# Second copies of keys and values for the other 64 partitions: loaded again, or copied by GpSimd

## The chip, the core and the metric

The kernel runs on one core of a Trainium2 chip. The metric is the device time of one execution in microseconds. A core has five engines, each with its own queue that it works off in order: TensorE (PE; its weight loads are shown as PEld), VectorE (DVE), ScalarE (ACT), GpSimd (POOL) and SyncE (SP). SP does nothing but issue transfers; GpSimd both computes and issues transfers, and both take their place in the same queue.

## What is computed

One layer of a decoder on 1024 tokens of 1024 channels. A combined input projection feeds a sliding-window attention with sinks, a gated linear recurrence and several gates; both branches are projected, merged, projected again and added to the input. The part that the change touches is the attention, 16 heads of 64 channels in 4 groups (one key and value head each), with a window of 128 tokens:

```python
s = jnp.einsum('bnqkgd,bnskd->bnkgqs', qb, kb) * (1.0 / math.sqrt(hd))
band = (diff >= 0) & (diff < WINDOW)
s = jnp.where(mask[None, :, None, None], s, -1e30)
m = jnp.maximum(jnp.max(s, axis=-1, keepdims=True), sink)
p = jnp.exp(s - m)
denom = jnp.sum(p, axis=-1, keepdims=True) + jnp.exp(sink - m)
o = jnp.einsum('bnkgqs,bnskd->bnqkgd', p / denom, vb)
```

All matmul operands are split into a high and a low part in fp32r, so that a product is made of three matmuls.

## The kernel before

The input projection runs in pieces of 12 matmuls (`piece()`, into banks `bk` of PSUM, later the recurrence's projection into `rp`). Into its last part the attention is woven: a loop over 35 *turns* u, of which turn u begins the block u (128 tokens of a group of four heads) and carries the two blocks before it further. TensorE's order in a turn is fixed by the order in which the code is written: `scores(u)` (tile `s_ps`, 8 matmuls of q against keys `ks`), the pieces, `values(u - 3)` (tile `pv`: weights `phc` and `plc` against `vb`, and `cm` against `vd`), `transposed(u - 2)` (tile `pt`), and then `scores(u + 1)`. `s_ps`, `pt` and `pv` have one buffer each.

Behind a transposition come, each on its own engine and in this order: ScalarE's cast `phc` (`split_a`), VectorE's difference `plc` (`split_d`), and two selects of GpSimd (`masks`), which write the halves of `cm` from `phc` and `plc`: partitions 64 to 127 of `cm` come from partitions 0 to 63 of `plc`. GpSimd's other work in a turn is `sink(u + 1)`, a small copy into the tile `p`, which waits for the transposition that frees the buffer.

A *pair* m is the two turns 2m and 2m+1, which share their keys, queries and values:

- `load_k(m)` writes `ks`, 64 channels in partitions 0 to 63 and the same again in 64 to 127 (the queries hold high parts in the one half and low parts in the other), in two transfers on SP's queue. It is called at the end of `scores(2m - 3)`.
- `load_v(m)` writes `vb` and `vd` in four transfers of 64 partitions on GpSimd's queue. In `vb` the upper half is the lower one shifted by one block of 64 tokens; in `vd` both halves are the same. It is called in `values(2m - 4)`, that is in turn 2m - 1, behind the masks of turn 2m - 2.

Stores of earlier results, such as `smr_d`, are on GpSimd's queue as well, where the pieces issue them: each waits for the ScalarE operation (`c`, L810) that makes its data.

Of the kernel before, what the change touches and what calls it, by code (L numbers as in the profile page):

```python
# [52 lines left out]
def tile_hybrid_block(ctx, tc, x, x_t, pk, rows, posr, posi, c_row, w_ss, w_gate, w_main, w_v,  # L53
                      w_g, w_ap, w_rp, w_out, out):
    nc = tc.nc
    V, A, G, T = nc.vector, nc.scalar, nc.gpsimd, nc.tensor

    def dma(dst, src, eng=nc.sync):
        dst, src = (a.bitcast(F32) if a.dtype == F32R else a for a in (dst, src))
        return eng.dma_start(dst, src)  # L60

    def f32(ap):
        return ap.bitcast(F32)
# [65 lines left out]
    vs_d = [tc.dram_tile([64, 18, P], F32, name=f"vs_d{g}") for g in range(NG)]  # L129
    dv_d = [tc.dram_tile([64, 18, P], F32, name=f"dv_d{g}") for g in range(NG)]  # L130
# [19 lines left out]
    for kc in range(KC):  # L150
        for lst, nm in ((hh, "hh"), (hl, "hl")):
            if kc < 4:
                a = hba.tile([P, HALF], F32R, name=f"{nm}a{kc}")
                b = b12.tile([P, HALF], F32R, name=f"{nm}b{kc}")
                lst.append([a[:], b[:]])
            else:
                a = hb.tile([P, S], F32R, name=f"{nm}{kc}")
# [641 lines left out]
    def flush():  # L799
        while behind:  # L800
            behind.pop(0)()
# [438 lines left out]

    at_ctx, psx_ctx = ExitStack(), ExitStack()
    at = psx = None
    U = {}

    def open_attn():
        nonlocal at, psx
# [14 lines left out]
    def load_k(m):  # L1261
        g, t0 = m // 4, (m % 4) * 256
        ks = at.tile([P, 2, 384], F32R, tag="ks", name="ks", bufs=2)
        kv = k_d.rearrange("(b a r j) t -> j (a r) b t", b=2, a=2, r=32, j=4)[g]
        lo = P if t0 == 0 else 0
        for rep in range(2):
            dma(ks[rep * 64:(rep + 1) * 64, :, lo:], kv[:, :, t0 - P + lo:t0 + 256])
        U["k", m] = ks

    def load_q(m):  # L1270
        g, t0 = m // 4, (m % 4) * 256
        qs = at.tile([P, 4, 256], F32R, tag="qs", name="qs", bufs=2)
        if g < 2:
            dma(qs[:], q_d[g][t0 // 64:t0 // 64 + 4].rearrange("x (a j) q -> a x (j q)", j=4))
        else:
            src = q_d[g].rearrange("(a j) t -> a j t", j=4)
            for i in range(4):
                dma(qs[:, i, :].rearrange("a (j q) -> a j q", j=4),
                    src[:, :, t0 + 64 * i:t0 + 64 * i + 64])
        U["q", m] = qs  # L1280

    def load_v(m):
        g, i0 = m // 4, m % 4 * 4
        vb = at.tile([P, 4, P], F32R, tag="vb", name="vb", bufs=3)
        vd = at.tile([P, 4, P], F32R, tag="vd", name="vd", bufs=3)
        for e in range(2):
            half = slice(64 * e, 64 * e + 64)
            dma(vb[half], vs_d[g][:, i0 + e:i0 + e + 4, :], G)
            dma(vd[half], dv_d[g][:, i0 + 2:i0 + 6, :], G)
        U["v", m] = vb, vd  # L1290

    def sink(u):
        px = at.tile([P, 4, P + 1], F32, tag="p", name="p", bufs=3)
        U["p", u] = px, at.tile([P, 2, 4], F32, tag="small", name="small", bufs=4)
        gs = W["sink"][:, u // 8 * 2:u // 8 * 2 + 2]
# [10 lines left out]
    def scores(u):  # L1306
        g, n = u // 8, u % 8
        ks, qs = U["k", u // 2], U["q", u // 2]
        s_full = psx.tile([P, 1024], F32, tag="s", name="s_ps")
        s_ps = s_full[:].rearrange("p (j k) -> p j k", j=4)  # L1310
        for j in range(4):
            h = j // 2
            t0 = (n % 2) * P + 64 * h
            first = 0 if n else P - 64 * h
            w = qs[:, n % 2 * 2 + h, j % 2 * P:j % 2 * P + P]
            for b in range(2):
                W["pe"] = T.matmul(s_ps[:, j, first:192], w, ks[:, b, t0 + first:t0 + 192],  # L1317
                                   start=(b == 0), stop=(b == 1))
        U["s", u] = s_ps, *U.pop(("p", u))
        if n % 2 and u // 2 + 2 < 16:  # L1320
            load_k(u // 2 + 2)
            load_q(u // 2 + 2)

    def maxima_a(u):
        s_ps, px, sm = U["s", u]
        if u % 8:
            A.copy(px[:, :, 0:P], s_ps[:, :, 0:P])
        else:
            A.copy(px[:, 2:4, 64:P], s_ps[:, 2:4, 64:P])

    def maxima_d(u):
        s_ps, px, sm = U["s", u]
        V.copy_predicated(px[:, :, 0:64], W["mle"][:].unsqueeze(1).to_broadcast([P, 4, 64]),
                          s_ps[:, :, P:192])
        V.tensor_reduce(out=sm[:, 0, :], in_=px[:], axis=AX.X, op=ALU.max, negate=True)

    def weights_a(u):
        s_ps, px, sm = U["s", u]
        for j in range(4):
            A.activation(px[:, j, :], px[:, j, :], AF.Exp, bias=sm[:, 0, j:j + 1],  # L1340
                         accum_out=sm[:, 1, j:j + 1])

    def weights_d(u):
        s_ps, px, sm = U["s", u]
        p, den = px[:, :, 0:P], sm[:, 1, :]
        V.reciprocal(den, den)
        V.tensor_tensor(out=p, in0=p, in1=den.unsqueeze(2).to_broadcast([P, 4, P]),
                        op=ALU.mult)

    def transposed(u):  # L1350
        px = U.pop(("s", u))[1]
        pt = psx.tile([P, 4, P], F32, tag="t", name="pt")
        for j in range(4):
            W["pe"] = T.transpose(pt[:, j, :], px[:, j, 0:P], ident[:])  # L1354
        U["t", u] = [pt]
# [6 lines left out]
    def split_d(u):  # L1362
        pt, phc = U.pop(("t", u))
        plc = at.tile([P, 4, P], F32R, tag="plc", name="plc")
        V.tensor_tensor(out=plc[:], in0=pt[:], in1=f32(phc[:]), op=ALU.subtract)
        U["m", u] = phc, plc
# [11 lines left out]
    def values(u):  # L1378
        vb, vd = U["v", u // 2]
        phc, plc, cm = U.pop(("m", u))  # L1380
        pv = psx.tile([P, 4, P], F32, tag="v", name="pv")
        prods = [(vb, m, h) for m in (phc, plc) for h in range(0 if u % 8 else 1, 2)]
        prods += [(vd, cm, h) for h in range(2)]
        for i, (b, m, h) in enumerate(prods):
            js = slice(2 * h, 2 * h + 2)
            W["pe"] = T.matmul(pv[:, js, :], b[:, u % 2 * 2 + h, :], m[:, js, :],  # L1386
                               start=(i == 0), stop=(i >= len(prods) - 2),
                               skip_group_check=True)
        if u % 2 == 0 and u // 2 + 2 < 16:
            load_v(u // 2 + 2)  # L1390
        U["pv", u] = [pv[:].rearrange("p (h a) (e q) -> p a e h q", h=2, e=2)]

    def join_a(u):
        pvv = U["pv", u][0]
        ob = at.tile([P, 2, P], F32, tag="ob", name="ob")
        obv = ob[:].rearrange("p a (h q) -> p a h q", h=2)
        A.copy(obv[0:64], pvv[64:128, :, 0])
        A.copy(obv[64:128], pvv[0:64, :, 1])
        U["pv", u].append(ob)
# [272 lines left out]
    def piece():  # L1672
        nonlocal left
        left -= 1
        next(more)

    late, high, loaded = [], [], {}
    for u in range(32 + 3):
        todo = (left - KEEP + (35 - u) // 2) // (35 - u)
        if u < 32:  # L1680
            scores(u)
            maxima_a(u)
            maxima_d(u)
            if u == 0:
                load_k(1)
                load_q(1)
                load_v(0)
            if u == 1:
                load_v(1)
        if 1 <= u < 33:  # L1690
            weights_a(u - 1)
        low = [steps_[2] for steps_ in high]
        while high:
            high.pop(0)[1]()
        for _ in range(todo):
            piece()
        flush()
        if 1 <= u < 33:
            weights_d(u - 1)
        if u >= 3:  # L1700
            values(u - 3)
            join_a(u - 3)
        if u >= 3:
            join_d(u - 3)
        if 2 <= u < 34:
            transposed(u - 2)
            split_a(u - 2)
            split_d(u - 2)
        if u + 1 < 32:
            sink(u + 1)()  # L1710
        if 2 <= u < 34:
            masks(u - 2)
        if "hpool" in W:
            for f in low:
                f()
            if late and ("gq", late[0]) in U and u >= loaded[late[0]] + 2:
                high.append(a_prep(late.pop(0)))
                high[0][0]()
        do_later()
        if u == 26:  # L1720
            outs(1)
        if u >= 3 and u % 2 == 0:
            late.append((u - 3) // 2)
        if u >= 2 and len(loaded) < 16 and len(loaded) <= (u - 2) // 2 and (
                len(loaded) - (late[0] if late else (u - 2) // 2) < 2):
            m = len(loaded)
            load_gq(m)
            loaded[m] = u
# [314 lines left out]
    for i in range(3):  # L2043
        f = fs[i]
# [8 lines left out]
    f = small()  # L2053
# [92 lines left out]
```

## Time and profile before

| what | value |
|---|---|
| time, median of 3 runs | 910.77 us (909.4 to 911.3) |
| time of the profiled execution | 906.86 us |
| its span | 905.1 us |
| TensorE busy | 882.7 us (98%) |
| VectorE busy | 721.7 us (80%) |
| ScalarE busy | 553.7 us (61%) |
| GpSimd busy | 183.4 us (20%) |
| moved by DMA | 183.12 MB, 202 GB/s over the span |

The attention's turns lie between 558 and 729 us of the span. In a row of the timeline the first number is the start in us, the second the duration in us, then the engine, the line of the kernel, the operation, what it writes and reads, its shape and how many instructions the row merges; a bracket gives the idle time of that engine just before, and what ended it. In a row of a group the bar separates the name and count from the busy time in us, the mean duration in ns, and the idle time before. DMA rows give the size of a transfer and the median time from its issue to its landing in us. Matmuls overlap, so the duration of a single one is longer than its share of the time.

### The profile page before, as it was taken

The page shows a single profiled execution, that of the slowest core. Times are in us where ns is not written, and L with a number is a line of the kernel's source. Part 1 is how long each engine was busy: PE and PEld are TensorE (multiplying, and loading weights), DVE is VectorE, ACT ScalarE, POOL GpSimd, SP SyncE. Part 2 cuts the span into 40 slices and gives each one's busy share as a digit, 9 for nine tenths or more (in the row PEclk, how much of TensorE's full clock was granted, in tenths as well). Part 3 has the DMA queues.
Part 4 walks back from the last instruction along what each step waited for, and adds up shares of the span by engine and source line. Part 5 has one row for each costly group of instructions (what it writes and reads, how often), then busy time and mean ns, then how long its engine had stood idle before and what let it go on. Part 6 is the DMA issues. An engine that isn't in the chain of part 4 may idle for free.

```text
span 905.1 us, 12954 instructions
## 1 busy us (share of the span) xinstructions
PE 882.7 (98%) x4235; PEld 737.6 (81%) x4235; DVE 721.7 (80%) x1166; ACT 553.7 (61%) x1099; POOL 183.4 (20%) x309
## 2 busy tenths in 40 slices
PE   5999999999999999999999999998999999999997
PEld 3879888888888788878887888887888888888886
DVE  7988798888669974986698476898999846779875
ACT  6754675554566746674777685877888631114555
POOL 0130232210110000000100003565665421310002
PEclk9999999999999999999999999999999999999999
DMA  9951885972534451344244246899889369869314
GB/s 350 414 187 63 292 248 194 311 246 93 181 134 139 149 200 34 137 148 170 104 164 169 82 152 208 280 330 296 222 229 259 122 209 328 297 253 325 141 47 185
DMA packets 99445, 183.12 MB, mean 202 GB/s; under 512 B 31329, under 2 KB 44129, under 8 KB 99378
## 3 DMA queue, kind: packets, MB, share of 16 engines
q1 hardware_dynamic: 86912, 144.52, 47.1%
q0 software_dynamic: 12176, 37.47, 12.5%
q8 instruction: 33, 0.54, 0.2%
q10 hardware_dynamic: 290, 0.32, 0.1%
q14 instruction: 34, 0.28, 0.1%
HBM read 127.37 MB, written 55.28 MB: 202 GB/s over the span
## 4 chain that ended last, share of the span: by engine, by line
PE 70%; DMA 11%; issue 8%; DVE 5%; ACT 4%; POOL 2%; SPq 0%; DVEq 0%; POOLq 0%; ACTq 0%
PE bk L707 39%; PE bo L1918 8%; PE rp L175 7%; PE pgate L1003 5%; DMA yl<-yl_d 3%; PE pmain L175 2%; PE s_ps L1317 2%; DMA r<-w_main 2%; PE pv L1386 2%; DMA wq<-w_out 2%; DMA hl<-yl_d 1%; DMA wq_d<-wq 1%; PE pt L1354 1%; PE bk L175 1%; DVE wl L110 1%
## 5 line engine op out<-in xcount | busy, mean ns | idle before, releaser
L707 PE MATMUL bk<-nh,wl 128*128 128x512 f32 x368 | 143.7, 390 | 0.4 <-DVE wl L110 0.4
L707 PE MATMUL bk<-nh,wh 128*128 128x512 f32 x368 | 143.3, 390 | 0.0
L707 PE MATMUL bk<-nl,wh 128*128 128x512 f32 x368 | 143.2, 389 | 0.0
L707 PEld LDWEIGHTS bk<-nh,wl 128*128 128x128 f32 x368 | 69.1, 188 | 16.1 <-DVE wl L110 1.9
L110 DVE TENSOR_TENSOR wl<-r,wh 128x512 fp32r<-128x512 f32 x112 | 81.4, 740 | 0.0
L707 PEld LDWEIGHTS bk<-nh,wh 128*128 128x128 f32 x368 | 69.1, 188 | 14.4
L707 PEld LDWEIGHTS bk<-nl,wh 128*128 128x128 f32 x368 | 69.1, 188 | 14.1
L60 POOL DMA_DIRECT2D wq_d<-wq x32 | 21.9, 684 | 270.4 <-DVE wq L1191 255.4
L104 ACT CAST wh<-r 128x512 fp32r<-128x512 f32 x112 | 68.0, 617 | 9.0 <-DMA r<-w_ap 6.3
L707 PE MATMUL bk<-hh,wl 128*128 128x512 f32 x184 | 71.7, 390 | 0.1
L707 PE MATMUL bk<-hh,wh 128*128 128x512 f32 x184 | 71.6, 389 | 0.0
L707 PE MATMUL bk<-hl,wh 128*128 128x512 f32 x184 | 71.6, 389 | 0.0
L110 DVE TENSOR_TENSOR wl<-ws,wh 128x512 fp32r<-128x512 f32 x80 | 54.5, 684 | 4.2 <-ACT wh L104 4.2
L1340 ACT ACTIVATE p<-p,small 128x129 f32<-128x129 f32 x128 | 50.1, 401 | 0.0
L104 ACT CAST wh<-ws 128x512 fp32r<-128x512 f32 x80 | 48.2, 614 | 2.9 <-PE bk L1570 2.7
L810 ACT ACTIVATE c<-bk 128x512 f32<-128x512 f32 x31 | 18.5, 597 | 44.3 <-PE bk L707 42.3
L707 PEld LDWEIGHTS bk<-hh,wl 128*128 128x128 f32 x184 | 34.5, 188 | 7.7 <-DVE wl L112 0.5
L707 PEld LDWEIGHTS bk<-hh,wh 128*128 128x128 f32 x184 | 34.6, 188 | 7.2
L707 PEld LDWEIGHTS bk<-hl,wh 128*128 128x128 f32 x184 | 34.5, 188 | 7.0
L1918 PE MATMUL bo<-wh,sum 128*128 128x512 f32 x128 | 39.6, 389 | 0.0
L1317 PE MATMUL s_ps<-ks,qs 128*128 128x192 f32 (+2 forms) x256 | 35.5, 281 | 2.1 <-DMA qs<-q_d 1.4
L707 PE MATMUL bk<-hha,wl 128*128 128x512 f32 x92 | 36.0, 392 | 0.6 <-DVE wl L110 0.6
(420 smaller groups left out, 2336.5 us busy)
## 6 DMA issues: line engine op xcount, KB each, us to landing
r<-w_main SPq DMA_DIRECT2D x100, 256.0 KB, 4.2
wada<-w_ss SPq DMA_DIRECT2D x16, 512.5 KB, 9.2
wq_d<-wq POOLq DMA_DIRECT2D x24, 256.0 KB, 3.0
wr<-wq_d SPq DMA_DIRECT2D x24, 256.0 KB, 4.8
ks<-k_d SPq DMA_DIRECT2D x24, 192.0 KB, 3.5
wg<-w_gate SPq DMA_DIRECT2D x8, 512.0 KB, 6.2
sma_d<-c POOLq DMA_DIRECT2D x16, 256.0 KB, 3.9
sgr_d<-c SPq DMA_DIRECT2D x16, 256.0 KB, 2.2
```

The costliest lines, as they stand in the source:

```text
L60: return eng.dma_start(dst, src)
L104: A.copy(dst[0][:], src)
L110: V.tensor_tensor(out=dst[1][:], in0=src, in1=f32(dst[0][:]), op=ALU.subtract)
L175: mm = T.matmul(ps[hf], ww, xx[kc][hf], start=(kc == first and ww is w_h and xx is xh), stop=(kc == last and xx is xl))
L707: W["pe"] = T.matmul(ps, ww[:, c], b[kc][xx_], start=(first and kc == 0 and i == 0), stop=(kc == 3 and i == 2), skip_group_check=not first)
L810: A.activation(t["t"], s(), AF.Tanh, scale=0.5)
L1003: W["pe"] = T.matmul(ps[:, SL[hf]], ww[:, c0:c0 + P], xx_[:, SL[hf]], start=(ic == 0 and i == 0), stop=(ic == 1 and i == 2))
L1317: W["pe"] = T.matmul(s_ps[:, j, first:192], w, ks[:, b, t0 + first:t0 + 192], start=(b == 0), stop=(b == 1))
L1340: A.activation(px[:, j, :], px[:, j, :], AF.Exp, bias=sm[:, 0, j:j + 1], accum_out=sm[:, 1, j:j + 1])
L1354: W["pe"] = T.transpose(pt[:, j, :], px[:, j, 0:P], ident[:])
L1386: W["pe"] = T.matmul(pv[:, js, :], b[:, u % 2 * 2 + h, :], m[:, js, :], start=(i == 0), stop=(i >= len(prods) - 2), skip_group_check=True)
L1918: T.matmul(bank[p][i] if dst is None else dst, a[:, ts_], b[:][:, sl], start=(new and kc == 0 and j == 0), stop=(kc == 3 and j == 2), skip ...
```

## The change

For the pairs from m = 2 on, `load_k` loads only the first 64 partitions, and a GpSimd copy makes the others; `load_v` loads the first half of `vb` and `vd`, and of the second half of `vb` only the last of its four blocks, and two GpSimd copies make the rest. The copies are not issued where the loads are, but kept in a table `twice` by turn: the keys' copy in turn 2m - 1, those of the values in turn 2m + 2, in both cases behind `split_d` and ahead of `sink` and `masks`.

```diff
@@ load_k
-        for rep in range(2):
+        for rep in range(2 if m < 2 else 1):
             dma(ks[rep * 64:(rep + 1) * 64, :, lo:], kv[:, :, t0 - P + lo:t0 + 256])
+        if m > 1:
+            twice.setdefault(2 * m - 1, []).append(
+                lambda: G.tensor_copy(ks[64:128, :, lo:], ks[0:64, :, lo:]))
@@ load_v
-        for e in range(2):
-            half = slice(64 * e, 64 * e + 64)
-            dma(vb[half], vs_d[g][:, i0 + e:i0 + e + 4, :], G)
-            dma(vd[half], dv_d[g][:, i0 + 2:i0 + 6, :], G)
+        a, b = slice(0, 64), slice(64, 128)
+        dma(vb[a], vs_d[g][:, i0:i0 + 4, :], G)
+        dma(vd[a], dv_d[g][:, i0 + 2:i0 + 6, :], G)
+        if m < 2:
+            dma(vb[b], vs_d[g][:, i0 + 1:i0 + 5, :], G)
+            dma(vd[b], dv_d[g][:, i0 + 2:i0 + 6, :], G)
+        else:
+            dma(vb[b, 3, :], vs_d[g][:, i0 + 4, :], G)
+            twice.setdefault(2 * m + 2, []).extend([
+                lambda: G.tensor_copy(vb[b, 0:3, :], vb[a, 1:4, :]),
+                lambda: G.tensor_copy(vd[b], vd[a])])
@@ the loop over turns, between split_d(u - 2) and sink(u + 1)
+        for f in twice.pop(u, ()):
+            f()
```

GpSimd's queue in an odd turn and the even one behind it, for m = 5 (turns 9 and 10; `vb<-vs_d` and `vd<-dv_d` are the transfers of `load_v`). Before:

```order
L60 DMA vb<-vs_d_90 64x512
L60 DMA vd<-dv_d_94 64x512
L60 DMA vb<-vs_d_90 64x512
L60 DMA vd<-dv_d_94 64x512
L1301 COPY p<-sink 128x4
L1372 AFFINE_SELECT cm<-phc 64x512
L1372 AFFINE_SELECT cm<-plc 64x512
L1301 COPY p<-sink 128x4
L1372 AFFINE_SELECT cm<-phc 64x512
L1372 AFFINE_SELECT cm<-plc 64x512
```

And after:

```order
L60 DMA vb<-vs_d_90 64x512
L60 DMA vd<-dv_d_94 64x512
L60 DMA vb<-vs_d_90 64x128
L1270 COPY ks<-ks 64x768
L1311 COPY p<-sink 128x4
L1382 AFFINE_SELECT cm<-phc 64x512
L1382 AFFINE_SELECT cm<-plc 64x512
L1298 COPY vb<-vb 64x384
L1299 COPY vd<-vd 64x512
L1311 COPY p<-sink 128x4
L1382 AFFINE_SELECT cm<-phc 64x512
L1382 AFFINE_SELECT cm<-plc 64x512
```

The keys' copy stands behind three transfers of the values, and the values' copies (those of the pair m = 4) stand ahead of the next sink copy and masks.

TensorE's queue at the end of turn 5 and the start of turn 6, with what its instructions wait for (DMAHW and DMASW are transfers of SP and of GpSimd, Pool is GpSimd). Before:

```order
L1386 MATMUL pv<-cm,vd 128x256 [waits DMASW6_49,DMASW0_49,Pool_49]
L1386 MATMUL pv<-cm,vd 128x256
L1354 MATMUL pt<-ident,p 128x128 [waits PE_49]
L1354 MATMUL pt<-ident,p 128x128 x3
L1317 MATMUL s_ps<-ks,qs 128x192 [waits DMAHW1_49,DMAHW2_49,DMAHW0_49,DVE_49]
```

And after:

```order
L1396 MATMUL pv<-cm,vd 128x256 [waits DMASW6_49,DMASW0_49,Pool_49]
L1396 MATMUL pv<-cm,vd 128x256
L1364 MATMUL pt<-ident,p 128x128 [waits PE_49]
L1364 MATMUL pt<-ident,p 128x128 x3
L1327 MATMUL s_ps<-ks,qs 128x192 [waits DMAHW0_49,DMAHW7_49,DVE_49,Pool_49]
```

The order on TensorE is the same; the scores of an even turn wait for one transfer less, and for GpSimd.

More of the change, by code (lines that the diff above doesn't have):

```diff
@@ L1242, in tile_hybrid_block @@
     at = psx = None
-    U = {}
+    U, twice = {}, {}
     def open_attn():
```

## The prediction

> **What bounds the kernel now.** I read the page's head first, then busy times by stretch, then TensorE's gaps, then one turn row by row.
>
> ```profile
> span 905.1 us, 12954 instructions
> PE 882.7 (98%) x4235; PEld 737.6 (81%) x4235; DVE 721.7 (80%) x1166; ACT 553.7 (61%) x1099; POOL 183.4 (20%) x309
> ```
>
> The whole program is bound by TensorE; GpSimd is busy for a fifth of it. The change touches only the attention stage, so its two halves are what counts (columns: start:end, length, then busy time and count of PE, PEld, DVE, ACT, POOL, granted clock, DMA share, GB/s).
>
> ```profile
> 560.00:640.00 80.00, 75.65 (x454) 65.94 (x453) 68.30 (x129) 64.69 (x207) 43.20 (x79) 1.00 0.93 280
> 640.00:720.00 80.00, 79.64 (x490) 70.73 (x489) 74.07 (x143) 68.12 (x222) 44.47 (x78) 1.00 0.78 220
> ```
>
> In the first half the DMA engines are 93% busy and TensorE loses 4.35 us; in the second it loses 0.36 us, at clock 1.00 in both. VectorE is idle for 11.7 and 5.93 us. These are all of TensorE's gaps there, with what ended each:
>
> ```profile
> 578.97 0.50 PE L1386 MATMUL pv<-cm,vd 128*128 128x256 f32 x2 [0.72 <-POOL cm L1372]
> 594.27 0.51 PE L1386 MATMUL pv<-cm,vd 128*128 128x256 f32 x2 [0.37 <-POOL cm L1372]
> 600.66 1.14 PE L1317 MATMUL s_ps<-ks,qs 128*128 128x192 f32 x8 [0.66 <-DVE p L1333]
> 616.89 1.11 PE L1317 MATMUL s_ps<-ks,qs 128*128 128x192 f32 x8 [1.41 <-DMA qs<-q_d]
> 621.50 0.73 PE L175 MATMUL rp<-yl,wh 128*128 128x512 f32 x2 [1.14 <-DMA yl<-yl_d]
> 718.07 0.50 PE L1386 MATMUL pv<-cm,vd 128*128 128x256 f32 x2 [0.36 <-POOL cm L1372]
> ```
>
> Loads cause 2.55 us of it. That is all that fewer bytes can win here, and the six gaps together, 4.66 us, are the most that any change of this stage's waits can win.
>
> **The change part by part: transfers removed.** For each of the 14 pairs of turns m = 2 to 15 one of the two loads of ks, the second load of vd and three quarters of the second load of vb go.
>
> ```profile
> ks<-k_d SPq DMA_DIRECT2D x24, 192.0 KB, 3.5
> vd<-dv_d POOLq DMA_DIRECT2D x32, 128.0 KB, 4.9
> ```
>
> That is 192 + 128 + 96 = 416 KB for a pair (352 KB for the three pairs with shorter keys), some 5.6 MB in all. Turns 9 and 12 begin with the s_ps at 600.66 and 616.89, so a pair takes 10.8 us there; at the first half's 280 GB/s 0.43 MB are 1.5 us of it, 14%. Some six pairs' loads lie ahead of the two load waits, 8 to 9 us of transfers, so I let both go: -2.55 us. SP issues one ks load less in a pair, which only lets its queue run earlier; GpSimd issues three v loads instead of four.
>
> **The ks copy.** It stands in GpSimd's queue in turn u = 2m-1, behind the masks of turn 2m-2 and behind the three v loads, and s_ps of turn 2m, the next thing that TensorE does after that turn's pv and pt, now waits for it. Turn 19 (m = 10) shows where that is: rows of four engines in order of the path, from the pt of turn 18 to the s_ps of turn 20.
>
> ```profile
> 651.58 0.60 PE L1354 MATMUL pt<-ident,p 128*128 128x128 f32 x4
> 653.50 0.69 DVE L1365 TENSOR_TENSOR plc<-pt,phc 128x512 fp32r<-128x512 f32 x1
> 654.32 0.98 POOL L1372 TENSOR_SCALAR_AFFINE_SELECT cm<-plc 64x512 fp32r<-64x512 f32 x1 [0.41 <-DVE plc L1365]
> 655.26 0.52 POOL L60 DMA_DIRECT2D vb<-vs_d  x1
> 655.77 0.53 POOL L60 DMA_DIRECT2D vd<-dv_d  x1
> 656.30 0.52 POOL L60 DMA_DIRECT2D vb<-vs_d  x1
> 656.82 0.52 POOL L60 DMA_DIRECT2D vd<-dv_d  x1
> 657.38 0.50 POOL L1301 COPY p<-sink 128x4 f32<-128x4 f32 x1
> 656.49 1.12 PE L1317 MATMUL s_ps<-ks,qs 128*128 128x192 f32 x8
> ```
>
> The loads' issues hold GpSimd one after the other: the sink copy starts only when the fourth is out. Three issues end at 655.26 + 1.57 = 656.83, already behind s_ps at 656.49, before the copy has begun. So the copy is not hidden here, whatever it costs.
>
> Its cost is not in the trace. The nearest rows are GpSimd's own:
>
> ```profile
> L1372 POOL TENSOR_SCALAR_AFFINE_SELECT cm<-plc 64x512 fp32r<-64x512 f32 x32 | 30.7, 959 | 16.6 <-DVE plc L1365 16.3
> L1372 POOL TENSOR_SCALAR_AFFINE_SELECT cm<-phc 64x512 fp32r<-64x512 f32 x32 | 21.2, 661 | 23.3 <-ACT phc L1359 23.2
> L1301 POOL COPY p<-sink 128x4 f32<-128x4 f32 x32 | 7.3, 230 | 25.4 <-PE pt L1354 23.0 <-issue 1.8
> L2033 POOL TENSOR_TENSOR xo<-xo,fg_bc 128x512 f32<-128x512 f32 x2 | 2.6, 1301 | 87.0 <-DMA out<-xo 87.0
> ```
>
> A select of 64x512 with one input, which also writes another half of the partitions in the plc form, takes 0.66 us undisturbed; the tiny copy shows some 0.2 us of fixed cost, which leaves 0.86 ns an element. A copy of 768 elements then takes 0.2 + 0.66, about 0.87 us, one of 512 (m = 4, 8, 12) 0.65 us. Bounds: 0.65 us for 768 (the select's whole time, if a copy streams a third faster), and 1.95 us (one and a half times the two-input operation's 1.30). I take 0.87, from the one-input row. The Trainium skill, GPSIMD Engine Reference, section 4.1, says that GpSimd runs one-input work at roughly line rate; as an estimate with the 1.2 GHz clock of its section 1, 768 elements would be 0.64 us, and the sum below some 2.5 us smaller. The select agrees in rate (0.86 ns an element).
>
> The stall of s_ps in a pair is therefore: start of the v loads + 1.57 + 0.87 - start of s_ps. The first three pairs, from the same two engines:
>
> ```profile
> 574.18 0.56 POOL L60 DMA_DIRECT2D smr_d<-c  x1 [1.82 <-ACT c L810]
> 574.74 0.53 POOL L60 DMA_DIRECT2D vb<-vs_d  x1
> 573.90 1.11 PE L1317 MATMUL s_ps<-ks,qs 128*128 128x192 f32 x8
> 584.84 0.53 POOL L60 DMA_DIRECT2D vb<-vs_d  x1
> 584.46 1.11 PE L1317 MATMUL s_ps<-ks,qs 128*128 128x192 f32 x8
> 594.44 0.53 POOL L60 DMA_DIRECT2D vb<-vs_d  x1 [0.22 <-issue]
> 594.97 1.09 PE L1317 MATMUL s_ps<-ks,qs 128*128 128x64 f32 x8
> ```
>
> - m = 2: GpSimd is held by the smr_d store, which waits for a ScalarE result of this very turn, so the v loads start behind s_ps: 574.74 + 2.44 - 573.90 = 3.28 us.
> - m = 3, held in the same way: 584.84 + 2.44 - 584.46 = 2.82 us.
> - m = 4 (512 elements): 594.44 + 2.22 - 594.97 = 1.69 us.
>
> For the other eleven (m = 5 to 15) the distance from the first v load to s_ps lies between these two, the longest (m = 7) and the shortest (m = 15):
>
> ```profile
> 626.47 0.52 POOL L60 DMA_DIRECT2D vb<-vs_d  x1
> 627.94 1.12 PE L1317 MATMUL s_ps<-ks,qs 128*128 128x192 f32 x8
> 703.87 0.53 POOL L60 DMA_DIRECT2D vb<-vs_d  x1
> 704.67 0.56 PE L1317 MATMUL s_ps<-ks,qs 128*128 128x192 f32 x3
> ```
>
> At 1.47 us of distance the stall is 0.97 us (0.75 with 512 elements), at 0.80 it is 1.64 (1.42). Nine long and two short copies give 10.2 us at the one end, 17.6 at the other. The short distances come from plc being late on VectorE, and a TensorE that stops once in a pair lets VectorE catch up; the 3.7 us from pt (651.58) to the mask's end (655.30) in the rows above hold the shortest form of that path, and it stays. I take 11.5 us, near the lower end. The stall recurs in every pair, since the path starts again at a pt that TensorE issues after the last stall.
>
> **The vb and vd copies.** Turn 2m+2 gets two, of 384 and 512 elements: 0.53 + 0.65 = 1.18 us, ahead of sink and masks. Ahead of the sink copy GpSimd mostly waits for pt (23.0 us in its row above), and that covers them: nothing. The exception is turn 6 (m = 2), where two smr_d stores leave no such wait: its masks end some 0.4 us later, and the gap at 594.27 grows and the copy for m = 4 starts later by as much: +0.4 us. Without that cover they would cost up to 1.18 us in each of 14 turns.
>
> **What the stalls take in.** While TensorE waits for a ks copy, what it later waited for gets done. The 0.72 us at 578.97 (masks some 0.3 us later, TensorE 3.3 us later) and the 0.66 us at 600.66 go; with the two loads -3.93 us.
>
> **VectorE and GpSimd together.** One weight preparation of VectorE, alone and beside a GpSimd mask:
>
> ```profile
> 599.56 0.68 DVE L110 TENSOR_TENSOR wl<-r,wh 128x512 fp32r<-128x512 f32 x1
> 654.71 1.14 DVE L110 TENSOR_TENSOR wl<-r,wh 128x512 fp32r<-128x512 f32 x1
> ```
>
> The second runs beside the mask of 654.32: it loses 0.46 us, and that mask takes 0.98 instead of 0.66. The 42 copies will cause more of this. The Trainium skill, SBUF — State Buffer, section "SBUF: two separate sides", says that VectorE work with two SBUF inputs and GpSimd work share a port pair as an exclusive lock, held for a whole instruction. The trace agrees: 1.14 against 0.68 us, and 0.98 against 0.66. By that rule alone the time would be that of the second rival below. In my sum this costs nothing, because each pair grows by more than 1 us and VectorE gets that as slack; as a bound of its own it is a rival.
>
> **Sum.** 3.28 + 2.82 + 1.69 + 0.4 + 11.5 - 3.93 = +15.8 us. The profiled execution took 906.86 us (span 905.1): 922.7. The median of the runs, 910.77, is 3.9 us above that execution, so the median after should be about 926 us.
>
> **Rivals.**
> - *The transfers decide (faster).* If the ks copy got in front of s_ps, the two load waits would go and nothing come back: 910.8 - 2.55 = 908.2; with 0.66 and 0.72 us more, 907. For it: DMA at 93% in the first half. Against: three issues alone end behind s_ps in turn 19. It decides only where masks end some 1 us earlier. 6 in 100.
> - *VectorE becomes the bound instead.* If the queue's stall were small and each copy held VectorE like a mask does, the second half would get 25 copies (turns 20 and 30 begin at 656.49 and 704.67, so 80 us hold 8.3 pairs of three) x 0.46 = 11.5 us against 5.93 us of idle time: +5.6; the first half's 18 copies (8.3 us) fit in its 11.7. With the loads' -2.55: +3 us, about 914. It begins where a copy costs VectorE more than 0.24 us. 7 in 100.
> - *Slow copies.* At 1.95 us instead of 0.87 for 768 elements, and 1.30 instead of 0.65, eleven and three of them add 13.8 us: 940. 8 in 100, as the tail of my own case.
> - *Gains and stalls cancel*: within 0.2%, 3 in 100.
>
> **Numbers.** My case, the queue's stall, has 84 in 100, its slow tail included; its own range is 918 to 940: 918 with copies of 0.65 us (-2.4), all eleven pairs at the lower end (-1.3) and the profiled execution as the base (-3.9), 940 as above. To take in the VectorE rival the range is 913 to 940. A change of under 0.2%, 1.8 us, can't be told from none here. Faster 6, same 3, slower 91 in 100.
>
> **What would show it.** Right: s_ps waits for GpSimd's ks copy in 14 turns, some 19 us in all, over 2.5 us in turns 4 and 6 and about 1 us from turn 10 on; the DMA waits of 616.89 and 621.50 are gone; ks copies of 64x768 near 0.87 us; VectorE's idle time in the stage grows. Wrong: s_ps doesn't wait for the copies; or it waits for VectorE (p, L1333); or copies far from 0.87 us, or slowed by VectorE to 1.3 us and more.

## The result and the profile after

The changed kernel took 925.0 us (median of 6 runs, 922.63 to 928.6), the kernel before 911.03 us beside it (6 runs, 906.3 to 911.86): a ratio of 1.0167, 95% interval 1.0142 to 1.0192. The profiled execution of the changed kernel took 922.63 us (span 920.9), 15.8 us more than that of the kernel before (906.86, span 905.1).

The head of the page after:

```profile
span 920.9 us, 12966 instructions
PE 886.4 (96%) x4235; PEld 740.5 (80%) x4235; DVE 726.5 (79%) x1166; ACT 554.2 (60%) x1099; POOL 206.8 (22%) x337
```

GpSimd has 28 instructions more and is still busy for only 22% of the span; TensorE's busy time has grown by 3.7 us in 15.8. The rest is waiting, and the view of TensorE's waits has one row for it (total, times, longest):

```profile
PE s_ps L1327 <- POOL ks L1270: 15.9, 14, 3.1
```

One wait in each of the 14 pairs, 15.9 us together. By the two halves of the stage (columns as in the prediction):

```profile
560.00:640.00 80.00, 70.51 (x412) 61.43 (x411) 63.07 (x118) 59.30 (x188) 47.54 (x81) 0.98 0.76 240
640.00:720.00 80.00, 74.40 (x457) 65.24 (x455) 70.09 (x129) 61.55 (x200) 56.11 (x94) 1.00 0.64 178
```

TensorE now loses 9.5 and 5.6 us where it lost 4.35 and 0.36, VectorE is idle for 17 and 10 us, the DMA engines' share falls from 0.93 and 0.78 to 0.76 and 0.64, and the clock is 0.98 in the first half. The first four of these waits and two of the later ones, in TensorE's timeline, with the one old gap that is left:

```profile
579.16 1.14 PE L1327 MATMUL s_ps<-ks,qs 128*128 128x192 f32 x8 [3.05 <-POOL ks L1270]
591.59 2.02 PE L1327 MATMUL s_ps<-ks,qs 128*128 128x192 f32 x8 [2.58 <-POOL ks L1270]
603.64 1.11 PE L1327 MATMUL s_ps<-ks,qs 128*128 128x64 f32 x8 [0.61 <-POOL ks L1270]
614.90 1.14 PE L1327 MATMUL s_ps<-ks,qs 128*128 128x192 f32 x8 [1.42 <-POOL ks L1270]
...
667.93 1.14 PE L1327 MATMUL s_ps<-ks,qs 128*128 128x192 f32 x8 [0.98 <-POOL ks L1270]
...
721.04 1.14 PE L1327 MATMUL s_ps<-ks,qs 128*128 128x192 f32 x8 [0.84 <-POOL ks L1270]
734.48 0.51 PE L1396 MATMUL pv<-cm,vd 128*128 128x256 f32 x2 [0.37 <-POOL cm L1382]
```

Of the six gaps of before (4.66 us) only the last one stands here, 0.37 us. The second row shows something else: 8 matmuls of the same shape take 2.02 us instead of 1.14. In windows of 2 us around it (length, busy time of TensorE, granted clock, DMA share, GB/s) that is the clock:

```profile
590.00:592.00 2.00, 0.41 (x2) 0.90 1.04 301
592.00:594.00 2.00, 2.00 (x10) 0.50 0.99 391
594.00:596.00 2.00, 2.00 (x8) 0.75 1.05 366
596.00:598.00 2.00, 2.00 (x16) 1.00 0.74 245
```

After the stop the clock is 0.50 for some 3.4 us, so that some 1.7 us are lost (0.2, 1.0 and 0.5 in the first three windows), and booked as busy time.

Turn 15 after, laid out like turn 19 in the prediction, shows the path that all these waits have in common (GpSimd's queue, then two rows of TensorE):

```profile
664.54 0.98 POOL L1382 TENSOR_SCALAR_AFFINE_SELECT cm<-plc 64x512 fp32r<-64x512 f32 x1 [0.41 <-DVE plc L1375]
665.48 0.52 POOL L60 DMA_DIRECT2D vb<-vs_d  x1
665.99 0.53 POOL L60 DMA_DIRECT2D vd<-dv_d  x1
666.52 0.52 POOL L60 DMA_DIRECT2D vb<-vs_d  x1
667.04 0.84 POOL L1270 CAST ks<-ks 64x768 fp32r<-64x768 f32 x1
666.35 0.60 PE L1364 MATMUL pt<-ident,p 128*128 128x128 f32 x4
667.93 1.14 PE L1327 MATMUL s_ps<-ks,qs 128*128 128x192 f32 x8 [0.98 <-POOL ks L1270]
```

From the end of the mask to the copy's end GpSimd never idles: three issues, then the copy. TensorE is through with pt at 666.95 and waits until 667.93.

From the start of the first s_ps to the start of the last pv the attention takes 185.22 us (560.02 to 745.24) instead of 170.75 (558.06 to 728.81): +14.5. The other 1.3 us lie outside it, where the programs are alike: it begins 2.0 us later, and what follows it is 0.6 us shorter.

### The profile page after: what moved, and what is told of

Same layout as the page of the kernel before. It is cut to its first block, busy times and chain, and to the rows that moved or that the text cites. A ratio compares the mean times of both kernels' runs of the same rounds, so it can differ in the third digit from the quotient of the medians.

```text
span 920.9 us, 12966 instructions
## 1 busy us (share of the span) xinstructions
PE 886.4 (96%) x4235; PEld 740.5 (80%) x4235; DVE 726.5 (79%) x1166; ACT 554.2 (60%) x1099; POOL 206.8 (22%) x337
## 4 chain that ended last, share of the span: by engine, by line
PE 74%; DVE 9%; ACT 5%; DMA 4%; issue 4%; POOL 3%; SPq 0%; ACTq 0%; DVEq 0%; POOLq 0%
PE bk L707 39%; PE rp L175 10%; PE bo L1930 8%; PE pmain L175 6%; PE pgate L1003 5%; PE s_ps L1327 2%; DVE wl L110 2%; DMA wada<-w_ss 1%; PE pv L1396 1%; PE bk L175 1%; DVE plc L1375 1%; DMA r<-w_main 1%; POOL vb L60 1%; POOL ks L1270 1%; PE bk L1580 1%
## 5 line engine op out<-in xcount | busy, mean ns | idle before, releaser
L1327 PE MATMUL s_ps<-ks,qs 128*128 128x192 f32 (+2 forms) x256 | 36.5, 286 | 15.9 <-POOL ks L1270 15.9
L1327 PEld LDWEIGHTS s_ps<-ks,qs 128*128 128x128 f32 x256 | 32.1, 196 | 19.5 <-POOL ks L1270 19.3
```

## The experiments

Each time stands against the kernel before on the same chip. The length of the attention is that of the profiled execution, from the start of the first s_ps to that of the last pv; "lost" is (1 - granted clock) x span, the mean over the runs.

| kernel | median us | ratio (95%) | attention us | wait for ks us, times | lost us |
|---|---|---|---|---|---|
| before (3 executions) | 909.65 to 911.03 | 1 | 170.75, 173.46, 170.81 | none | 1.9 to 2.2 |
| after (2 executions) | 925.0 | 1.0167 (1.0142 to 1.0192) | 185.22, 186.77 | 15.9, 14 | 5.1 |
| e1_values_only | 905.48 | 0.9958 (0.994 to 0.9976) | 167.74 | none | 1.6 |
| e2_key_first | 908.44 | 0.9993 (0.9975 to 1.001) | 170.09 | 2.9, 3 | 1.6 |
| e3_key_after_masks | 905.81 | 0.9955 (0.9935 to 0.9975) | 168.18 | 0.3, 1 | 2.0 |
| e4_no_copies | 904.0 | 0.9943 (0.9926 to 0.9961) | 167.00 | none | 1.6 |
| e5_key_copy_double | 956.01 | 1.0509 (1.0467 to 1.055) | 215.77 | 29.5, 14 | 23.4 |
| e6_keys_only | 941.05 | 1.0335 (1.0298 to 1.0372) | 203.08 | 24.2, 14 | 12.7 |
| e7_from_pair_4 | 919.83 | 1.0102 (1.0042 to 1.0162) | 180.53 | 10.5, 12 | 2.8 |
| e8_from_pair_3 | 920.53 | 1.0114 (1.0073 to 1.0156) | 181.92 | 13.0, 13 | 4.6 |
| e9_keys_only_after_masks | 907.27 | 0.9974 (0.9958 to 0.999) | 169.08 | 0.3, 1 | 1.5 |

**Only the values copied.** Keys are loaded twice as before; the values' copies and the transfers they replace stay changed.

```diff
-        for rep in range(2 if m < 2 else 1):
+        for rep in range(2):
...
-        if m > 1:
+        if m > 99:
```

> Keys loaded twice as before, values copied as after. Theory (place in GpSimd's queue): without the keys' copy no s_ps waits for GpSimd, the 15.9 us of such waits go, and the time falls back to the kernel before less what the lighter DMA wins, 907 to 911 us. Rival (GpSimd copies slow VectorE through a shared port, whatever their place): 28 of the 42 copies are left, so two thirds of the loss stay, about 920 us.

It is 0.4% faster than before, and 1.5 us under the expected range. No s_ps waits for GpSimd. TensorE's gaps in the stage are 0.69, 0.50, 0.22 and 0.37 us, and only the first has copies ahead of it, in turn 6 (some rows of it):

```profile
594.65 0.55 POOL L60 DMA_DIRECT2D smr_d<-c  x1 [0.39 <-ACT c L810]
595.64 0.63 POOL L1299 CAST vd<-vd 64x512 fp32r<-64x512 f32 x1
596.47 0.65 POOL L1382 TENSOR_SCALAR_AFFINE_SELECT cm<-phc 64x512 fp32r<-64x512 f32 x1
598.23 0.50 PE L1396 MATMUL pv<-cm,vd 128*128 128x256 f32 x2 [0.69 <-POOL cm L1382]
```

There GpSimd goes from the store through the copies to the masks without a pause, where before the first mask still waited 0.38 us for ScalarE and the gap was 0.37 us. Elsewhere the values' copies are hidden, as forecast, and the slowdown hangs on the keys' copy alone.

**The keys' copy ahead of the three transfers of the values.** In turn 2m-1, still behind the smr_d stores.

```diff
-            twice.setdefault(2 * m - 1, []).append(
+            twice.setdefault(("k", 2 * m - 1), []).append(
...
+        for f in twice.pop(("k", u), ()):
+            f()
         if u >= 3:
             values(u - 3)
```

> The changed kernel with the keys' copy ahead of the three value transfers instead of behind them, all else the same. Theory: the copy ends 1.57 us earlier, so the stalls of about 0.85 us of the later pairs vanish, those of turns 4 and 6 shrink from 3.05 and 2.58 to about 1.5 and 1.0 us, since the smr_d store is still ahead, and TensorE's clock is not halved: s_ps waits 2 to 3 us in all, 908 to 912 us. Rival (the copy itself costs, through its 0.87 us or through VectorE): as after, 920 us and more.

The same copies, three issues earlier. Groups of GpSimd and TensorE's waits:

```profile
L1270 POOL CAST ks<-ks 64x768 fp32r<-64x768 f32 x11 | 10.9, 993 | 0.0
PE s_ps L1327 <- POOL ks L1270: 2.9, 3, 1.5
```

The copies take longer than in the changed kernel (993 against 870 ns, the row for that is below), and yet 11 of 14 waits are gone and the other three shrink to 1.51, 1.12 and 0.27 us. So in most pairs the copy, even a longer one, ends in time once the 1.57 us of issues are not ahead of it in GpSimd's queue. The copy's own length counts as well where it stands behind them (see the copy made twice).

**The keys' copy right behind the masks of turn 2m-2**, ahead of the smr_d stores too.

```diff
-            twice.setdefault(2 * m - 1, []).append(
+            twice.setdefault(("k", 2 * m - 2), []).append(
...
         if 2 <= u < 34:
             masks(u - 2)
+        for f in twice.pop(("k", u), ()):
+            f()
```

> The changed kernel with the keys' copy issued one place earlier still, behind the masks of turn 2m-2, so ahead of the smr_d store too. Theory: no s_ps waits for a copy any more, the DMA waits of 1.41 and 1.14 us stay gone: 906 to 909 us, faster than before by 2 to 4 us. Rival (VectorE is held by the copies): 913 us or more, with s_ps waiting for VectorE. A third possibility: the copies wait for the keys to land in the first half and push the masks back: pv waits for cm, 911 to 914.

This version beats both kernels: 905.81 us, 0.45% under the kernel before and 2.1% under the changed one. One wait for a copy is left:

```profile
PE s_ps L1327 <- POOL ks L1270: 0.3, 1, 0.3
```

**The transfers left out and no copies.** The buffers are fixed, and what the other 64 partitions hold, of the keys from the third pair on and of the values from the fourth, is left over from earlier pairs.

```diff
-        ks = at.tile([P, 2, 384], F32R, tag="ks", name="ks", bufs=2)
+        ks = KB[m % 2]
...
-        vb = at.tile([P, 4, P], F32R, tag="vb", name="vb", bufs=3)
-        vd = at.tile([P, 4, P], F32R, tag="vd", name="vd", bufs=3)
+        vb, vd = VB[m % 3]
...
-        if m < 2:
+        if m < 3:
...
-        for f in twice.pop(u, ()):
-            f()
+        twice.pop(u, ())
```

> The transfers that the change removes are left out and no copies are made; the upper halves keep what the first pairs loaded (so part of the keys and values is that of other blocks). What fewer bytes are worth by themselves: theory 906.5 to 908.5 us, the two DMA waits of 2.55 us gone and little else. If the transfers were hidden anyway: 911.

The missing bytes alone are worth 5.6 us by the medians, more than the 3.93 of the prediction and more than expected here. And e3 stands 1.8 us above this: by the medians that is the whole price of 42 copies, 33 us of GpSimd's time, where they lie well. The intervals of the two ratios overlap, so that the 1.8 us are not told apart from nothing.

**The keys' copy made twice.**

```diff
         for f in twice.pop(u, ()):
             f()
+            if u % 2:
+                f()
```

> The changed kernel with every keys' copy made twice, one behind the other. Theory: the copy lies fully on the path to s_ps, so each of the 14 stalls grows by the copy's own time, 11 x 0.87 + 3 x 0.63 = 11.5 us: 936 us, and 2 us more for each further halving of TensorE's clock. Rival (the copies are hidden, and something else makes the change slow): 925 to 927 us.

The waits grow as they should: 29.5 us, 13.6 more, 0.97 for a pair, where a copy takes 0.89. The time grows by 31 us, more than twice that. The rest is in the granted clock, here at two stops, in a window of 2 us behind each, and over 40 us:

```profile
665.36 1.11 PE L1327 MATMUL s_ps<-ks,qs 128*128 128x64 f32 x8 [1.55 <-POOL ks L1270]
668.00:670.00 2.00, 2.00 (x6) 0.50 0.14 49
678.52 1.14 PE L1327 MATMUL s_ps<-ks,qs 128*128 128x192 f32 x8 [1.71 <-POOL ks L1270]
680.00:682.00 2.00, 2.00 (x10) 1.00 0.40 136
640.00:680.00 40.00, 35.03 (x187) 0.87 0.51 136
```

Behind the stop of 1.55 us the clock is halved, behind that of 1.71 us it is not. The mean of 0.87 also holds a half clock behind 1.71 us at 652.37 and the end of one behind 2.24 us at 639.20; the changed kernel with stops of about 0.9 us keeps 1.00 (640 to 720). Lost time is 23.4 us against 5.1 of the changed kernel: 18.3 us, which with the 13.6 us of waits make 31.9.

**Only the keys copied**, so that four transfers of the values stand ahead of the copy.

```diff
-        if m < 2:
+        if True:
             dma(vb[b], vs_d[g][:, i0 + 1:i0 + 5, :], G)
```

> Keys copied as after, values loaded twice as before, so that four value transfers stand ahead of the keys' copy instead of three. Theory: every stall grows by the one issue, 14 x 0.53 = 7.4 us: 931 to 934 us, slower than after though the copies of the values are gone. Rival (the values' copies carry a good part of the loss): below 922 us.

The fourth issue adds 8.3 us of waits, 0.59 for a pair; an issue takes 0.52. Another 7.6 us is clock (12.7 lost against 5.1 of the changed kernel). One queue entry of half a microsecond, 14 times, makes some 16 us, more than twice the 7.4 expected, though the values' copies are gone here and their second loads are back.

**The keys' copy only from pair 4 on, and only from pair 3 on.** Two kernels that take the long stalls away, the first both, the second that of m = 2.

```diff
-        for rep in range(2 if m < 2 else 1):
+        for rep in range(2 if m < 4 else 1):
...
-        if m > 1:
+        if m > 3:
```

> The changed kernel, but the keys of the pairs 2 and 3 are loaded twice as before. Theory: the stalls of 3.05 and 2.58 us go, and with them the halved clock that followed (1.8 us): 917 to 919 us, no half clock in the attention. If the half clock had another cause than the stall: 919 to 921 us with a half clock still there.

```diff
-        for rep in range(2 if m < 2 else 1):
+        for rep in range(2 if m < 3 else 1):
...
-        if m > 1:
+        if m > 2:
```

> The changed kernel, but the keys of pair 2 alone are loaded twice. The 3.05 us stall goes, the one of 2.6 us in turn 6 stays. If that one alone is enough to halve TensorE's clock: 921 to 923 us with a half clock behind it; if the clock falls only where two long stalls follow within some 12 us: 919 to 921 us and clock 1.00 throughout the attention.

The question was whether two long stops in a row are needed for the half clock. First two rows of the kernel from pair 4, then one of that from pair 3:

```profile
595.86 0.51 PE L1396 MATMUL pv<-cm,vd 128*128 128x256 f32 x2 [0.65 <-POOL cm L1382]
598.01 1.68 PE L1327 MATMUL s_ps<-ks,qs 128*128 128x64 f32 x8 [1.21 <-POOL ks L1270]
...
586.30 2.00 PE L1327 MATMUL s_ps<-ks,qs 128*128 128x192 f32 x8 [2.60 <-POOL ks L1270]
```

They are not, and the idea that the clock holds once the long stops are away falls. A single stop of 2.60 us halves the clock (2.00 us for eight matmuls that take 1.14), and even 0.65 and 1.21 us within 3 us do (1.68 instead of 1.11). The four runs of the kernel from pair 4 stand in the order of their clocks: 914.95 us at 0.999, 919.29 and 920.36 at 0.997, 923.88 at 0.995. But the lost time grows only from 0.9 to 4.6 us over these 8.9, so the clock is not all that differs between them; what else does is open.

**Again the kernel before, twice, and the changed one**, to see what a second and a third execution look like.

> The kernel before once more, for a second trace. The lighter DMA won 4 to 6 us where 2.55 us of DMA waits stood in the first trace, whose execution was among the fastest. Theory: the DMA waits of TensorE between 560 and 640 us differ from execution to execution, and this one shows 3 to 7 us of them, or a half clock behind one. Rival: the same 2.5 us, and the rest of the win is somewhere else.

> As the run ahead of it: a third trace of the kernel before, with the same expectations.

> The changed kernel once more. Theory: the same 14 waits for the keys' copy, 15 to 17 us, with one to three half clocks behind them, 1.8 us each; a lower mean clock goes with a longer span. Rival: the half clock of the first trace was an accident, and the clock is 1.00 here throughout the attention.

before_2 (911.45 us, span 909.7) has the half clock too. Its two load waits, and the clock behind them:

```profile
617.84 1.11 PE L1317 MATMUL s_ps<-ks,qs 128*128 128x192 f32 x8 [1.53 <-DMA qs<-q_d]
623.41 1.20 PE L175 MATMUL rp<-yl,wh 128*128 128x512 f32 x2 [2.16 <-DMA yl<-yl_d]
...
624.00:626.00 2.00, 2.00 (x10) 0.50 1.07 354
626.00:628.00 2.00, 2.00 (x14) 0.78 0.40 143
```

The load waits are 3.69 us here instead of 2.55, and a half clock follows; the attention takes 173.46 us, 2.7 more than in the first execution. before_3 (908.98 us) has 1.42 and 1.28 us at clock 1.00, and 170.81. In after_2 (922.95 us) the waits for ks are those of the first execution within 0.03 us, but the clock is halved behind the first stop as well as the second:

```profile
577.88 1.63 PE L1327 MATMUL s_ps<-ks,qs 128*128 128x192 f32 x8 [3.05 <-POOL ks L1270]
578.00:580.00 2.00, 2.00 (x10) 0.58 0.88 334
```

In the first execution of the changed kernel the window of 578 to 580 stands at 1.00, behind the same 3.05 us. Same program, same stop, and another clock: 1.55 us of the attention's length.

**Only the keys copied, behind the masks of turn 2m-2**: the place of e3 with the values loaded twice.

> Keys copied, behind the masks of turn 2m-2; values loaded twice as before. Theory: no stall, and the share of the win that the keys' transfers carry: 906 to 908 us, behind the versions with the values copied as well or equal to them. Rival (the win comes from the values' transfers alone, which are on GpSimd's queue): 909 to 910 us, as before.

907.27 us, 2.6 us under the kernel before: the keys' transfers alone win over half of what e3 does (3.8). The values' alone win 4.2 (e1), so the two shares do not simply add up. The same part of the change costs 31 us in e6 and wins 2.6 here, by its place in one queue.

## Why the prediction was right, point by point

- **The ks copy behind three issues: right.** The wait exists in all 14 pairs with the path that the prediction laid out, and moving the copy ahead of the issues takes nearly all of it away (e2, e3). The copies' durations in the changed kernel, by group:

```profile
L1270 POOL CAST ks<-ks 64x768 fp32r<-64x768 f32 x11 | 9.6, 870 | 0.0
L1270 POOL CAST ks<-ks 64x512 fp32r<-64x512 f32 x3 | 1.9, 625 | 0.0
L1298 POOL CAST vb<-vb 64x384 fp32r<-64x384 f32 x14 | 10.1, 723 | 0.0
```

  870 and 625 ns, against 0.87 and 0.65 us taken from the select. (The working had a slip: 0.66 less 0.2 us over 512 elements is 0.90 ns, not 0.86; for 768 elements that makes 0.03 us.) The estimate of 0.64 us for 768 elements, which the prediction worked out from the Trainium skill (GPSIMD Engine Reference, sections 1 and 4.1), is reached by none of the copies of that size, of which the shortest takes 0.84 us here.

- **The two long stalls: right.** 3.28 and 2.82 us forecast, 3.05 and 2.58 measured. In both GpSimd waited for the smr_d store first; with the copy ahead of that store (e3) they are gone, with it behind (e2) 1.51 and 1.12 us are left.

- **m = 4: mis-sized.** 1.69 us and 0.4 for the late masks forecast, 0.61 measured (0.61 in after_2, 0.62 in e8). The prediction took the distance from the first v load to s_ps from the trace of before, 0.53 us. In the changed kernel the v loads start at 601.32, and TensorE is through at 603.03, a distance of 1.71: behind two stalls and a half clock on TensorE the other engines have had time to catch up. The kernel from pair 4, with no such stall ahead, supports it: 1.21 us there, with 0.65 us of waiting for cm just before. The prediction applied this very argument to the gaps of before and to the eleven later pairs, but not to this one. Of the 0.4 us for turn 6's masks nothing shows in the changed kernel, where the first mask waits 0.30 us for ScalarE behind the copies; with no stall ahead the term is there, as a gap of 0.65 to 0.69 us (e1, e3, e7) in place of 0.37.

- **The eleven others: 11.5 us forecast, 9.69 measured**, just under the lower end of 10.2. The reason given for staying near that end holds in ten of them: the distance in turn 15 above is 1.47 us, the longest of before, and the ten lie between 1.46 and 1.72. Only m = 5 keeps a short one, 1.05 us, with a stall of 1.42. Distances longer than any of before, which the sum did not have, did the rest.

- **The gaps that go: forecast 3.93 us, 4.29 in the trace** (4.66 less the 0.37 that stays). But the median gain of e4 is 5.6. The attention of before takes 170.75 to 173.46 us, that of e4 167.00: 3.75 us in the execution that the prediction read, 6.5 in before_2, where the load waits are longer and halve the clock. The execution that was read showed the cheapest of three, and its ceilings of 2.55 us for fewer bytes and 4.66 us for all waits hold for it alone. e4's remaining 1 us or so may lie behind the attention (175.7 us from there to the end, against 176.3 to 177.8); what ends it there was not tried.

- **The clock: a term that was not in the sum.** Some 1.7 us in the first execution of the changed kernel, and over its six runs 5.1 us lost against 2.2. It made up for the stalls, which came out smaller: 15.9 of waits - 4.3 + 1.7 make 13.3 us of the attention's 14.5. The other 1.2 us, 0.13 for each of nine stops more than before, may be the time until the matmuls flow again; no run measured that by itself. The agreement of 926 and 925.0 is thus partly luck: stalls 3.8 us under their forecast, and some 3 us that the sum did not have. So is that of 15.8 us between the two profiled executions, 1.3 us of which lie outside the attention.

- **The rivals.** VectorE as the bound falls: in e1 and e3 the copies run beside it (two thirds or all of the 42), and the kernels are faster than before. Transfers deciding did not happen in this order of the queue, but it is what e3 shows: forecast 907 to 908.2 for that case, measured 905.81. The condition named for it, masks that end 1 us earlier, was one way; three issues less ahead of the copy are another. Slow copies: not seen alone. e5, with 13.6 us more of waits, shows about what they would have cost: 956, not 940, since the clock goes with them.

## What to carry to other kernels

What an operation adds to an engine's busy time says little; what stands ahead of it in that engine's queue, issues of transfers among it, and who waits behind it decide: the same keys' copies with their transfers cost 31 us behind four issues and win 2.6 ahead of them. Before a store or a load is judged harmless on an idle engine, count its half microsecond on the queue against the distance to the reader. And a stop of TensorE is priced with the clock behind it: in this kernel a stop of over a microsecond could bring 1.7 us of lost clock with it, more than a stop of 1.55 us itself, and only several executions show how often.

## What was not expected of the hardware

- **The half clock after stops shorter than expected.** Stops of 2.58, 2.60 and 2.16 us, and 0.65 with 1.21 us, were each followed by some 3.4 us at a clock of 0.50. Read in windows of 0.5 us, every such stretch in the attention loses the same 1.71 us, whatever the stop ahead, but for one of twice that (behind 3.91 us in e5). Over the attention of all 14 traces a stretch goes with 13 of the 14 stops of over 2 us and with 11 of the 33 of 1 to 2 us, so in these runs the length of a stop alone does not decide it. The same 3.05 us stop halved the clock in one execution and not in another. The Trainium skill (TensorE: Matmul & The Clock Gate, "What's actually happening") says that activity is judged in windows of some 3.4 us that run free of the program. That the same stop has two outcomes agrees with it, and so does the length of 3.4 us. The rule that the same page of the Trainium skill gives for kernels ("HAM oscillation — how this bites in real kernels"), no idle gaps over about 3.4 us, is too generous here.
- **GpSimd beside VectorE.** In e3 a copy of 64x384 takes 0.50 us at its shortest and 0.95 at its longest, one of 64x768 0.82 and 1.27. The long ones looked at run beside VectorE's work with two inputs: that of 1.27 us at 610.32 starts inside a weight preparation of 1.14 us from 609.76. This fits the lock that the prediction spoke of, and yet all 42 copies cost 1.8 us by the medians where next to nothing waits for them.
